# Layer 1's input projection by Strassen's algorithm in a two-layer encoder step

## The chip, the cores and the metric

The kernel runs on one core of a Trainium2 chip. The metric is the device time of one execution, in microseconds (us). The engines are named as in the profile: PE is TensorE (matmuls; PEld its weight loads), DVE is VectorE, ACT is ScalarE, POOL is GpSimd, SP is SyncE, whose queue issues all of this kernel's DMAs.

## The reference

One inference step of a two-layer trunk of width 1024 for 1024 prompt positions and 64 sample positions. Layer 0 is sparse attention beside a short convolution; the change leaves it alone. Layer 1, the "odd" mixer, is what matters here:

```python
def _odd_mixer(h, w_in, ws, bs, ln_g, ln_b, w_out):
    u, v, g = _split(h @ w_in, (SGU_DIM, SGU_DIM, SGU_DIM))
    u = jax.nn.gelu(u)
    v = _layernorm(jax.nn.gelu(v), ln_g, ln_b)
    ...
    s = jnp.einsum('gij,bnjgc->bnigc', wm, vc) + bs[:, :lc].T[None, None, :, :, None]
    s = s.reshape(nb, T, SGU_DIM)
    out = (u * s * jax.nn.silu(g)) @ w_out
    return out, v
...
        x = x + gate[:, None] * out
    ...
    return _rmsnorm(x, final_g), ...
```

`h` is the scaled and shifted RMS norm of x, `w_in` is 1024 x 3072, all data are float32. `wm` is a lower-triangular 128 x 128 matrix for each of 8 channel groups; it mixes positions inside blocks of 128. The normalised v of the 64 sample positions is an output of its own.

## The kernel before, in words

Activations lie transposed: channels on the 128 partitions in `KT` = 8 tiles, `TC` = 1088 columns for the positions (1024 prompt, 64 sample). Each float32 operand of a projection is split into a rounded high part and the rest, `ah` and `al` for the activations, `w_hi` and `w_lo` for the weights; a product is high x high + high x low + low x high, so three matmuls for each of the 8 channel tiles (`product`, L261). `project` makes one column tile of 128 outputs in three chunks of 364, 364 and 360 columns: 72 matmuls. `weights` loads a raw tile of 512 KB (L127), lets ACT round it (L252) and POOL subtract (L253); there are two raw buffers.

Layer 0 ends with its output projection (`out_projection`, three chunks `OUT_CHUNKS` of 448, 384 and 256 columns). Behind each matmul group DVE adds the gated result to the residual x (L1150), ACT squares it and POOL sums the squares; `rstd` makes the norm, and `h1` writes layer 1's `ah` (ACT, L1175) and `al` (POOL makes the float32 value, L1174, DVE subtracts, L1176). The residual stays in SBUF until the end.

`layer1` then runs 24 column tiles in the order v, g, u. For v: gelu, then PE transposes each 128 x 128 block into `vtok` (position on the partitions), copied out of PSUM by DVE (L1259); DVE does the layer norm (`layernorm`: statistics, scaling, times `ln_g`, plus `ln_b`). For g: silu into `gs`. `spatial` makes the mix, one group of channels at a time, by 8 + 1 matmuls, adds the bias and multiplies into `gs` (DVE, L1218, L1220). For u: gelu (ACT, L1289), multiplied into `gs` (DVE, L1290). At last `gs` is split into `ah` and `al` (L292, L293) and the second output projection runs, with `final` (L1182) behind it.

PSUM has eight banks, given out by tags: `pj`, `lg`, `pt` twice each, `av` and `x` once. Each engine runs its instructions strictly in the order in which they stand. That order is fixed when the program is built: for most of the program a scheduler places each instruction by estimated times, so an instruction written later may stand earlier.

Of the kernel before, what the change touches and what calls it, by code (L numbers as in the profile page):

```python
# [17 lines left out]
P = 128  # L18
# [77 lines left out]
OUT_KTS = (4, 5, 6, 7, 0, 1, 2, 3)  # L96

# [7 lines left out]
class Trunk:  # L105
# [1027 lines left out]
    def out_projection(self, l, ws, after):  # L1133
# [4 lines left out]
        for c in range(NCH):  # L1138
# [3 lines left out]
            acc = self.tmp.tile([P, CW], F32, tag="acc", name="acc", bufs=2)[:, 0:w]  # L1142
            for t in range(KT):
# [8 lines left out]
                if t == 0:  # L1152
                    nc.scalar.activation(acc, x[:, t, :], AF.Square)
                else:
                    sq = self.tmp.tile([P, CW], F32, tag="hf1", name="sq", bufs=2)[:, 0:w]
                    nc.scalar.activation(sq, x[:, t, :], AF.Square)  # L1156
                    if t < KT - 1 or c < NCH - 1:
                        nc.gpsimd.tensor_add(acc, acc, sq)  # L1158
                if c and t == 1:
                    after(c - 1, self.rstd("rstd", *accs[c - 1]))  # L1160
            accs.append((w, acc) if c < NCH - 1 else (w, acc, sq))
        after(NCH - 1, self.rstd("rstd", *accs[-1]))

    def h1(self, c, rb):
        nc = self.nc
        a0, b0 = OUT_CHUNKS[c]
        w = b0 - a0
        for kt in range(KT):
            t = self.tmp.tile([P, CW], F32, tag="t1", name="t1", bufs=2)[:, 0:w]
            hf = self.tmp.tile([P, CW], F32, tag="hf1", name="hf1", bufs=2)[:, 0:w]  # L1170
            nc.vector.tensor_mul(t, self.xc[c][:, kt, :], rb)
            for j, a, b in self.spans(c):
                sc, sh = self.modA[1][:, kt, j:j + 1], self.mod[1][:, kt, j:j + 1]
                nc.gpsimd.tensor_scalar(hf[:, a:b], t[:, a:b], sc, sh, op0=OP.mult, op1=OP.add)  # L1174
                nc.scalar.activation(self.ah[:, kt, a0 + a:a0 + b], t[:, a:b], AF.Identity, scale=sc, bias=sh)  # L1175
            nc.vector.tensor_sub(self.al[:, kt, a0:b0], hf, self.ah[:, kt, a0:b0])  # L1176
# [13 lines left out]
    def layernorm(self, n, pool):  # L1190
        nc = self.nc
        r = slice(0, P) if n < NBLK else slice(0, DEC)
        v = self.vtok[r, n, :]
        st = self.small.tile([P, 2, 6], F32, tag="bn", name="bn", bufs=2)
        mv = self.small.tile([P, 4], F32, tag="mv", name="mv", bufs=2)
        for i in range(2):
            nc.vector.bn_stats(st[r, i, :], v[:, i * 512:(i + 1) * 512])
# [7 lines left out]
    def spatial(self, g):  # L1205

        nc = self.nc
        pt = [self.bank("lg", "sgu_ps") for _ in range(2)]
        for n in range(NBLK):
            nc.tensor.matmul(pt[n // 4][:, (n % 4) * P:(n % 4 + 1) * P], self.vtok[:, n, g * P:(g + 1) * P],  # L1210
                             self.wm[:, g, :], start=True, stop=True)
        ps = self.bank("av", "sgus_ps")
        nc.tensor.matmul(ps[:, 0:DEC], self.vtok[0:DEC, NBLK, g * P:(g + 1) * P], self.wm[0:DEC, g, 0:DEC],
                         start=True, stop=True)
        gs = self.gs
        for a in range(2):
            s = self.big.tile([P, 512], F32, tag="sgu", name="sgu", bufs=1)
            nc.vector.tensor_add(s.rearrange("p (b c) -> p b c", c=P), pt[a].rearrange("p (b c) -> p b c", c=P),  # L1218
                                 self.bs[:, g, None, :].to_broadcast([P, 4, P]))
            nc.vector.tensor_mul(gs[:, g, a * 512:a * 512 + 512], gs[:, g, a * 512:a * 512 + 512], s)  # L1220
        s = self.small.tile([P, DEC], F32, tag="sgus", name="sgus", bufs=2)
        nc.vector.tensor_add(s, ps[:, 0:DEC], self.bs[:, g, 0:DEC])
        nc.vector.tensor_mul(gs[:, g, SO:SO + DEC], gs[:, g, SO:SO + DEC], s)

    def layer1(self):
# [3 lines left out]
        with ExitStack() as es:  # L1229
            gp = es.enter_context(self.pool("gates", "right"))  # L1230
            self.gs = gs = gp.tile([P, KT, TC], F32, name="gs")
            with ExitStack() as e2:
                b = e2.enter_context(self.pool("sgu", "right"))
                self.vtok = b.tile([P, NBLK + 1, D], F32, name="vtok")
                with self.pool("ln", "right") as lp:
                    self.lng, self.lnb = lp.tile([P, D], F32, name="lng"), lp.tile([P, D], F32, name="lnb")
                    with self.tc.issue_after(self.lastload):
                        self.load(self.lng, i["ln_g"].partition_broadcast(P))
                        self.load(self.lnb, i["ln_b"].partition_broadcast(P))
                    def gelu(t):  # L1240
                        def evac(c, ps):
                            nc.scalar.activation(gs[:, t, slice(*CHUNKS[c])], ps, AF.Gelu_apprx_tanh)
                        return evac


                    two = [self.weights(w1[t]) for t in range(2)]
                    for t in range(2):
                        self.project(two[t], gelu(t), range(NCH - 1))
                    for t in range(KT):
                        if t < 2:  # L1250
                            self.project(two[t], gelu(t), (NCH - 1,))
                        else:
                            self.project(self.weights(w1[t]), gelu(t))
                        for a in range(2):
                            pt = self.bank("lg", "v_ps")
                            for n in range(4):
                                nc.tensor.transpose(pt[:, n * P:(n + 1) * P],
                                                    gs[:, t, (4 * a + n) * P:(4 * a + n + 1) * P], self.ident)
# [12 lines left out]
                self.load(self.bs.rearrange("p g c -> p (g c)"), i["bs"].partition_broadcast(P))
                nc.gpsimd.affine_select(out=self.wm, in_=self.wm, compare_op=OP.is_ge, fill=0.0, base=0,
# [136 lines left out]
```

## Time and profile before

| What | us |
|---|---|
| median of 3 runs (lowest, highest) | 1114.68 (1113.75, 1117.47) |
| the profiled execution, its own time | 1114.53 |
| its span, first to last instruction | 1112.8 |
| layer 1's input projection starts, on PE | 689.63 |
| second output projection starts, on PE | 1004.25 |
| last matmul group of the output projection ends | about 1102 |

The granted PE clock was 0.994 of full speed over the span. In a timeline row the columns are start, duration, engine, line and operation; a matmul's duration overlaps the next one's, so the pace is the distance between starts. In a row of grouped instructions the columns are busy us, mean ns of one, and the engine's idle time before them with what ended it.

### The profile page before, as it was taken

How to read it: one execution, taken by the hardware profiler on the slowest of the kernel's cores; microseconds unless marked ns; L12 is line 12 of the kernel's file. 1: busy time of each engine (PE TensorE's matmuls, PEld its weight loads, DVE VectorE, ACT ScalarE, POOL GpSimd, SP SyncE). 2: the span in 40 equal slices, each digit the busy share in tenths (PEclk: the TensorE clock that was granted, in tenths of full speed). 3: DMA queues.
4: the chain of work that ended last, by engine and by line, in shares of the span. 5: the costliest groups of instructions: out<-in, count | busy, mean ns of one | idle time of the engine just before them, and what ended most of it. 6: DMA issues, size and time to landing. Idle time of an engine off the chain costs nothing.

```text
span 1112.8 us, 18831 instructions
## 1 busy us (share of the span) xinstructions
PE 1077.3 (97%) x7255; PEld 1042.8 (94%) x7255; DVE 645.6 (58%) x1614; ACT 535.4 (48%) x1019; POOL 440.9 (40%) x463
## 2 busy tenths in 40 slices
PE   5899999999999999999999999999999999999996
PEld 4889778999999989999999999999999999999996
DVE  5611789998887777677785344311492082346134
ACT  5643588766776687677785234411221112144111
POOL 1014223356675566455374356411242101264222
PEclk9999999999999999999999999999999999999998
DMA  9755601211010110000003501111112101130012
GB/s 370 285 199 170 238 30 57 79 39 56 22 39 24 63 48 21 20 20 20 20 20 108 205 1 38 39 38 38 39 48 95 39 20 39 46 125 20 1 67 95
DMA packets 25786, 81.84 MB, mean 74 GB/s; under 512 B 3040, under 2 KB 9440, under 8 KB 23264
## 3 DMA queue, kind: packets, MB, share of 16 engines
q1 hardware_dynamic: 25696, 80.63, 20.4%
q8 instruction: 57, 0.93, 0.3%
q14 instruction: 33, 0.27, 0.1%
HBM read 74.50 MB, written 6.12 MB: 72 GB/s over the span
## 4 chain that ended last, share of the span: by engine, by line
PE 88%; DVE 6%; ACT 4%; issue 2%; DMA 0%; POOL 0%; POOLq 0%; DVEq 0%; ACTq 0%
PE pj L261 44%; PE op L261 15%; PE pj L278 9%; PE av L728 3%; PE logit_ps L684 3%; PE p_ps L710 3%; PE ada_ps L165 2%; PE first L333 2%; PE sgu_ps L1210 1%; PE score_ps L448 1%; DVE cum L644 1%; PE score_ps L449 1%; DVE al L293 1%; ACT rel L451 1%; DVE bias L645 1%
## 5 line engine op out<-in xcount | busy, mean ns | idle before, releaser
L261 PE MATMUL pj<-ah,w_hi 128*128 128x364 f32 (+1 forms) x984 | 326.0, 331 | 1.0 <-ACT w_hi L252 1.0
L261 PE MATMUL pj<-al,w_hi 128*128 128x364 f32 (+1 forms) x984 | 323.8, 329 | 0.0
L261 PE MATMUL pj<-ah,w_lo 128*128 128x364 f32 (+1 forms) x984 | 323.0, 329 | 0.0
L253 POOL TENSOR_TENSOR w_lo<-w_raw,w_hi 128x1024 fp32r<-128x1024 f32 x63 | 155.5, 2469 | 345.8 <-ACT w_hi L252 343.8
L261 PEld LDWEIGHTS pj<-ah,w_hi 128*128 128x128 f32 x984 | 185.0, 188 | 2.0 <-ACT w_hi L252 1.3
L261 PEld LDWEIGHTS pj<-ah,w_lo 128*128 128x128 f32 x984 | 184.9, 188 | 0.3 <-issue 0.2
L261 PEld LDWEIGHTS pj<-al,w_hi 128*128 128x128 f32 x984 | 185.1, 188 | 0.0
L252 ACT ACTIVATE w_hi<-w_raw 128x1024 fp32r<-128x1024 f32 x68 | 71.8, 1058 | 108.0 <-PE pj L261 86.6
L550 DVE TENSOR_SCALAR_CACHE_REDUCE junk<-S,cand 128x512 bf16<-128x512 f32 (+5 forms) x142 | 119.0, 838 | 1.9
L261 PE MATMUL op<-al,w_hi 128*128 128x256 f32 (+2 forms) x344 | 112.0, 326 | 0.5 <-DVE al L293 0.5
L261 PE MATMUL op<-ah,w_hi 128*128 128x256 f32 (+2 forms) x344 | 112.3, 327 | 0.0
L261 PE MATMUL op<-ah,w_lo 128*128 128x256 f32 (+2 forms) x344 | 111.6, 326 | 0.0
L278 PE MATMUL pj<-ah,w_hi 128*128 128x364 f32 (+1 forms) x288 | 95.5, 332 | 0.0
L278 PE MATMUL pj<-ah,w_lo 128*128 128x364 f32 (+1 forms) x288 | 95.4, 331 | 0.0
L278 PE MATMUL pj<-al,w_hi 128*128 128x364 f32 (+1 forms) x288 | 95.2, 330 | 0.0
L577 ACT ACTIVATE junk<-S,cand 128x896 bf16<-128x896 f32 (+2 forms) x78 | 77.7, 996 | 30.3 <-DVE m L580 26.4
L1150 DVE SCALAR_TENSOR_TENSOR x<-op,mod,x 128x192 f32<-128x192 f32 (+2 forms) x64 | 30.2, 497 | 101.6 <-PE op L261 97.0
L691 POOL TENSOR_SCALAR S<-S,sm 128x128 f32<-128x128 f32 (+8 forms) x68 | 51.6, 763 | 67.5 <-DVE sm L690 54.8
L1158 POOL TENSOR_TENSOR acc<-acc,sq 128x448 f32<-128x448 f32 (+2 forms) x40 | 40.7, 1019 | 86.2 <-ACT sq L1156 85.5
L1156 ACT ACTIVATE sq<-x 128x448 f32<-128x448 f32 (+2 forms) x42 | 21.3, 506 | 96.5 <-DVE x L1150 92.9
L261 PEld LDWEIGHTS op<-al,w_hi 128*128 128x128 f32 x344 | 64.9, 189 | 2.6 <-DVE al L293 0.9
L261 PEld LDWEIGHTS op<-ah,w_hi 128*128 128x128 f32 x344 | 64.9, 189 | 1.7
(254 smaller groups left out, 2080.0 us busy)
## 6 DMA issues: line engine op xcount, KB each, us to landing
w_raw<-in_w SPq DMA_DIRECT2D x53, 512.0 KB, 3.4
ada<-in_ada_w SPq DMA_DIRECT2D x19, 1024.0 KB, 7.7
w_raw<-in_wo SPq DMA_DIRECT2D x16, 512.0 KB, 3.5
x<-in_x SPq DMA_DIRECT2D x8, 544.0 KB, 6.0
bo<-in_ada_w SPq DMA_DIRECT2D x4, 1024.0 KB, 6.8
x<-in_x SPq DMA_DIRECT2D x1, 1792.0 KB, 8.1
out_y<-x SPq DMA_DIRECT2D x1, 1792.0 KB, 6.6
x<-in_x SPq DMA_DIRECT2D x1, 1536.0 KB, 7.7
```

Of the source, the lines that this page charges most:

```text
L252: nc.scalar.activation(hi, raw, AF.Copy)
L253: (nc.gpsimd if lo_eng == "pool" else nc.vector).tensor_sub(lo, raw, hi)
L261: last = self.nc.tensor.matmul(ps, wt[:, kt, :], at[:, kt, c0:c1], start=n == 0, stop=n == len(mms) - 1)
L278: self.nc.tensor.matmul(ps, wt[:, kt, :], at[:, kt, a:b], start=kt == 0 and i == 0, stop=kt == KT - 1 and i == 2)
L550: V.tensor_scalar(junks[0][:, 0:SW[j]], self.S[:, span(j)], thr, 0.0, op0=OP.is_lt, op1=OP.add, accum_out=col(cv, j))
L577: nc.scalar.activation(junks[1][:, 0:SW[j]], self.S[:, span(j)], AF.Sign, scale=-1.0, bias=col(cand, j), accum_out=col(cv, j))
L684: nc.tensor.matmul(pt[:, 0:w], lhs, keys[i][:, t // 2, s], start=i == 0, stop=i == 1)
L691: self.lastnorm = nc.gpsimd.tensor_scalar(p, p, st[:, 3:4], 0.5, op0=OP.mult, op1=OP.mult).ins
L710: nc.tensor.transpose(pt[0:r, o:o + P], p[:, j * P:j * P + r], self.ident)
L728: self.lastav = nc.tensor.matmul(av[:, 0:m], self.vs[0:r, vbase + j, t // 2, :], part[0:r, x:x + m], start=j == 0 and i == 0, stop=(j + 1) ...
L1150: nc.vector.scalar_tensor_tensor(x[:, t, a:b], ps[:, a:b], self.mod[l][:, 16 + t, j:j + 1], x[:, t, a:b], op0=OP.mult, op1=OP.add)
L1158: nc.gpsimd.tensor_add(acc, acc, sq)
```

## The change

For 22 of the 24 column tiles of the input projection, two neighbouring tiles are made together by Strassen's algorithm (in the form with seven products). The weights of a pair are taken as a 2 x 2 matrix: two column tiles by the two halves of the channels (4 tiles of 128, `KH`). The activations are 2 x 2 too: halves of the channels by two neighbouring blocks of `Q` = 272 columns; there are two such groups of columns (`q`). Each of the seven products is a sum of weight quarters times a sum of activation quarters, over half the channels: 3 x 4 = 12 matmuls of 272 columns for each q. The results are added up in SBUF.

- The activation sums T1, T2, T3 and T4 are made once for all pairs: `sums` makes them in place of h, which `h1` now keeps in x's own buffers, and `sum_parts` splits them into high and low parts. T4 takes the place of a quarter of `ah` and `al`.
- For each pair DVE makes the four weight sums, ACT and POOL split seven weight quarters into four slots in turn (`pair_weights`).
- `pair` adds each product out of PSUM (DVE, 14 additions a pair; one copy for each q on ACT), applies gelu or silu in SBUF, and, for pairs from t = 12 on, multiplies into `gs` (`times`, DVE).
- The residual x is copied to DRAM behind its last update in layer 0's output projection (`spill`) and loaded again for layer 1's.
- The layer norm now only subtracts the mean and divides (ACT); `ln_g` multiplies behind the mix, and `ln_b` goes into the bias `bs` through the column sums of `wm` (`mix`, two more matmuls). The sample rows of v get both directly for the output.
- Layer 1's output weights for six of the eight tiles go into the places of T2, T1 and T3.

```diff
 def out_projection ...
+            if l == 0:
+                self.load(self.spill[c], x)
 def h1 ...
-                nc.gpsimd.tensor_scalar(hf[:, a:b], t[:, a:b], sc, sh, op0=OP.mult, op1=OP.add)
+                nc.gpsimd.tensor_scalar(x[:, kt, a:b], t[:, a:b], sc, sh, op0=OP.mult, op1=OP.add)
...
+    def sums(self):
+        V = self.nc.vector
+        for _, n, (c1, o1), (c2, o2) in self.half_pieces():
+            b11, b21 = (self.xc[c1][:, k:k + KH, o1:o1 + n] for k in (0, KH))
+            b12, b22 = (self.xc[c2][:, k:k + KH, o2:o2 + n] for k in (0, KH))
+            V.tensor_sub(b11, b12, b11)
+            V.tensor_sub(b12, b22, b12)
+            V.tensor_sub(b22, b22, b11)
+            V.tensor_sub(b21, b21, b22)
...
+    def pair_weights(self, s1, s2):
...
+        def parts(src):
+            self.turn += 1
+            w = pool.tile([P, 2, KH, P], F32R, tag=("whi0", "wlo0", "whi1", "wlo1")[self.turn % 4], name="p_w")
+            nc.scalar.activation(w[:, 0], src, AF.Copy)
+            nc.gpsimd.tensor_sub(w[:, 1], src, w[:, 0])
+            return w
...
+        yield parts(a11)
+        yield parts(a12)
+        t1 = total(0, V.tensor_add, a21, a22)
+        t2 = total(1, V.tensor_sub, t1, a11)
+        yield parts(t2)
+        yield parts(total(2, V.tensor_sub, a11, a21))
+        yield parts(t1)
+        yield parts(a22)
+        yield parts(total(0, V.tensor_sub, a12, t2))
+
+    def pair(self, t, dst, f, done=None, mid=None):
...
+        for n, (w, b) in enumerate(zip(ws, ("B11", "B21", "T2", "T3", "T1", "T4", "B22"))):
+            for q in range(2):
+                tag = ("pj", "lg", "pt")[n % 3]
+                ps = self.ps.tile([P, 512], F32, tag=tag, name="st", bufs=2)[:, 0:Q]
+                hi, lo = self.quarter(b, q)
+                mms = [(0, at, k) for k in range(KH) for at in (hi, lo)] + [(1, hi, k) for k in range(KH)]
+                for i, (p, at, k) in enumerate(mms):
+                    nc.tensor.matmul(ps, w[:, p, k, :], at[:, k, :], start=i == 0, stop=i == len(mms) - 1)
...
+                if n == 0:
+                    nc.scalar.activation(x12, ps, AF.Copy)
+                elif n == 1:
+                    V.tensor_add(x11, x12, ps)
+                    finish(0, s1)
...
+                else:
+                    V.tensor_add(x12, x12, ps)
+                    finish(0, s2)
...
 def layernorm ...
-        nc.vector.tensor_scalar(v, v, mv[r, 0:1], mv[r, 2:3], op0=OP.subtract, op1=OP.mult)
-        nc.vector.tensor_mul(v, v, self.lng[r])
-        nc.vector.tensor_add(v, v, self.lnb[r])
+        nc.vector.scalar_tensor_tensor(mv[r, 3:4], mv[r, 0:1], -1.0, mv[r, 2:3], op0=OP.mult, op1=OP.mult)
+        for i in range(2):
+            v = self.vtok[i][r, n, :]
+            nc.scalar.activation(v, v, AF.Identity, scale=mv[r, 2:3], bias=mv[r, 3:4])
 def spatial ...
+            nc.vector.scalar_tensor_tensor(o, p, self.lngb[:, 0, g:g + 1], b, op0=OP.mult, op1=OP.add)
+            if times:
+                nc.vector.tensor_mul(y, y, u)
 def layer1 ...
+        for t in range(2, KT, 2):
+            mid = transposes(t - 2, v)
+            v = [ring((t + n) % 4) for n in range(2)]
+            self.pair(t, v, AF.Gelu_apprx_tanh, mid=mid)
...
+        self.pair(KT, gsa, AF.Silu, mid=mix)
+        gsa += [ring(n) for n in range(2, 4)]
+        self.pair(KT + 2, gsa[2:], AF.Silu)
+        for g in range(4):
+            self.spatial(g, gsa[g], True)
...
+        for g in range(4, KT):
+            self.spatial(g, gs[g], False)
...
+        self.load(xc[0], self.spill[0])
...
+        for n, t in enumerate((*range(KT + 4, 2 * KT, 2), *range(2 * KT, 3 * KT, 2))):
+            def times(src, k, s):
+                nc.vector.tensor_mul(gs[t % KT + k][:, s], gs[t % KT + k][:, s], src)
+            self.pair(t, [tmp[:, n % 2 * 2 + k, :] for k in range(2)],
+                      AF.Silu if t < 2 * KT else AF.Gelu_apprx_tanh, done=times)
```

Up to the first chunk of `h1` every engine's instructions stand as before. Three places of DVE's order, each before and after:

**The end of h.** Before, DVE's last lower parts of h (L1176; `hf` is the float32 value) are followed at once by the copies of the first transposes.

```order
L1176 TENSOR_TENSOR al<-hf_7846,ah 128x256
L1176 TENSOR_TENSOR al<-hf_7854,ah 128x256
L1176 TENSOR_TENSOR al<-hf_7862,ah 128x256
L1259 COPY vtok<-v_ps 128x4x128 x3
L1263 COPY vtok<-vs_ps 64x128
```

Now DVE has the sums there (L1221 to L1223; `x_6978` is the last chunk of x, `x_6980` the one before) and the low parts of T3, T2 and T4, then the first pair's first addition (L1304) and weight sums (`p_s`).

```order
L1181 TENSOR_TENSOR al<-x_6978,ah 128x256
L1221 TENSOR_TENSOR x_6978<-x_6978 128x1024
L1222 TENSOR_TENSOR x_6978<-x_6978,x_6980 128x1024
L1223 TENSOR_TENSOR x_6980<-x_6980,x_6978 128x4x256
L296 TENSOR_TENSOR T3l<-x_6978,T3h 128x4x256
L296 TENSOR_TENSOR T2l<-x_6978,T2h 128x4x256
L296 TENSOR_TENSOR al<-x_6980,ah 128x4x256
L1304 TENSOR_TENSOR ring<-ring,st 128x272
L1263 TENSOR_TENSOR p_s<-p_raw 128x512 x2
L1332 COPY vtok_8087<-v_ps 128x4x128 x2
```

Six operations of 1024 columns have come between the last part of h and the weight sums, and the copies of the transposes have moved behind them.

**The end of the norm.** Before, DVE's order runs through the scaling of the last blocks (L1201 to L1203) into the mix (L1218).

```order
L1201 TENSOR_SCALAR vtok<-vtok,mv 128x1024 x2
L1202 TENSOR_TENSOR vtok<-vtok,lng 128x1024
L1198 BN_AGGR mv<-bn 128x2
L1202 TENSOR_TENSOR vtok<-vtok,lng 128x1024
L1203 TENSOR_TENSOR vtok<-vtok,lnb 128x1024
L1199 TENSOR_SCALAR mv<-mv 128x1
L1203 TENSOR_TENSOR vtok<-vtok,lnb 128x1024
L1201 TENSOR_SCALAR vtok<-vtok,mv 128x1024
L1202 TENSOR_TENSOR vtok<-vtok,lng 128x1024
L1203 TENSOR_TENSOR vtok<-vtok,lnb 128x1024
L1218 TENSOR_TENSOR sgu<-sgu_ps,bs 128x512
```

Now the statistics (L1344 to L1348) stand between the additions of a pair (L1315, L1318), and the last of them behind the mix's first operation (L1372).

```order
L1344 BN_STATS bn<-vtok_8087 128x6
L1344 BN_STATS bn<-vtok_8088 128x6
L1318 TENSOR_TENSOR ring<-ring,st 128x272
L1348 SCALAR_TENSOR_TENSOR mv<-mv 128x1
L1345 BN_AGGR mv<-bn 128x2
L1346 TENSOR_SCALAR mv<-mv 128x1
L1318 TENSOR_TENSOR ring<-ring,st 128x272
L1348 SCALAR_TENSOR_TENSOR mv<-mv 128x1
L1372 SCALAR_TENSOR_TENSOR sgu<-sgu_ps,lngb,misc 128x512
L1345 BN_AGGR mv<-bn 128x2
L1374 TENSOR_TENSOR ring<-ring,sgu 128x512
```

Three operations of 1024 columns for each block have left DVE, and the rest has moved to just before the mix.

**The end of a gate pair.** Before, DVE had one multiplication for each chunk of a tile, `u` being a new buffer each time.

```order
L1290 TENSOR_TENSOR gs_7874<-gs_7874,u_9744 128x364
L1290 TENSOR_TENSOR gs_7874<-gs_7874,u_9772 128x364
L1290 TENSOR_TENSOR gs_7874<-gs_7874,u_9800 128x360
L1290 TENSOR_TENSOR gs_7874<-gs_7874,u_9834 128x364
L1290 TENSOR_TENSOR gs_7874<-gs_7874,u_9862 128x364
```

Now, at the end of the pair t = 12 (the results of products 5 and 6 are `st_9874` to `st_9922`, and `st_10001` belongs to the next pair):

```order
L1315 TENSOR_TENSOR u_9688<-u_9688,st_9874 128x272
L1466 TENSOR_TENSOR gsb_9625<-gsb_9625,u_9688 128x272
L1315 TENSOR_TENSOR u_9688<-u_9688,st_9890 128x272
L1466 TENSOR_TENSOR gsb_9625<-gsb_9625,u_9688 128x272
L1318 TENSOR_TENSOR u_9688<-u_9688,st_9906 128x272
L1466 TENSOR_TENSOR gsb_9625<-gsb_9625,u_9688 128x272
L1318 TENSOR_TENSOR u_9688<-u_9688,st_9922 128x272
L1466 TENSOR_TENSOR gsb_9625<-gsb_9625,u_9688 128x272
L1263 TENSOR_TENSOR p_s_10206<-p_raw_10187 128x512
L1304 TENSOR_TENSOR u_9688<-u_9688,st_10001 128x272
```

Each addition is now followed by the multiplication of its own result, with a function on ACT between the two, and the addition that frees the last bank (L1318) stands behind a multiplication.

More of the change, by code (lines that the diff above doesn't have):

```diff
@@ L1207, in spatial @@
+    def spatial(self, g, gs, times):
         nc = self.nc
-        pt = [self.bank("lg", "sgu_ps") for _ in range(2)]
+        vt, c = self.vtok[g // 4], slice(g % 4 * P, (g % 4 + 1) * P)
+        pt = [self.ps.tile([P, 512], F32, tag="lg", name="sgu_ps", bufs=2) for _ in range(2)]
         for n in range(NBLK):
-            nc.tensor.matmul(pt[n // 4][:, (n % 4) * P:(n % 4 + 1) * P], self.vtok[:, n, g * P:(g + 1) * P],
-                             self.wm[:, g, :], start=True, stop=True)
-        ps = self.bank("av", "sgus_ps")
@@ L1213, in spatial @@
[L1213 to L1225, printed above, removed]
+            nc.tensor.matmul(pt[n // 4][:, (n % 4) * P:(n % 4 + 1) * P], vt[:, n, c], self.wm[:, g, :],
+                             start=True, stop=True)
+        ps = self.ps.tile([P, 512], F32, tag="x" if g % 2 else "av", name="sgus_ps", bufs=1)
@@ L1226, in layer1 @@
+    def layer1(self, es):
         nc = self.nc
@@ new lines, in layer1, with ring, gelu, evac @@
+        r1 = es.enter_context(self.pool("sums", "right"))
+        self.T = {t: [r1.tile([P, KH, 2 * Q], F32R, tag=f"T{t}{x}", name=f"T{t}{x}") for x in "hl"] for t in (1, 2, 3)}
+        def ring(n):
+            return r1.tile([P, TC], F32, tag=f"ring{n}", name="ring")
+        v = [ring(n) for n in range(2)]
+        def gelu(t):
+            def evac(c, ps):
+                nc.scalar.activation(v[t][:, slice(*CHUNKS[c])], ps, AF.Gelu_apprx_tanh)
+            return evac
+        two = [self.weights(w1[t]) for t in range(2)]
@@ new lines, in layer1, with mix @@
+        gsa = [ring(n) for n in range(2)]
+        mid = transposes(KT - 2, v)
+        def mix():
+            mid()
+            for a in range(2):
+                ps = self.ps.tile([P, 512], F32, tag="av" if a else "x", name="r_ps", bufs=1)
+                nc.tensor.matmul(ps, ones, misc[:, 2, a * 512:a * 512 + 512], start=True, stop=True)
+                for g in range(4 * a, 4 * a + 4):
+                    nc.vector.scalar_tensor_tensor(self.bs[:, g, :], ps[:, g % 4 * P:(g % 4 + 1) * P],
+                                                   self.lngb[:, 1, g:g + 1], self.bs[:, g, :], op0=OP.mult, op1=OP.add)
+            for n in (NBLK, *range(NBLK)):
+                self.layernorm(n)
+            for h in range(2):
+                x = slice(h * 512, h * 512 + 512)
+                nc.vector.tensor_mul(lng[0:DEC, x], lng[0:DEC, x], self.vtok[h][0:DEC, NBLK, :])
+            nc.vector.tensor_add(lng[0:DEC], lng[0:DEC], lnb[0:DEC])
+            self.load(self.o["cv"], lng[0:DEC])
@@ new lines, in layer1 @@
+        ws = [self.weights(i["wo1"][t], "pool", place=r1.tile([P, 2, KT, P], F32R, tag=f"T{(2, 1, 3)[t // 2]}{'hl'[t % 2]}",
+                                                             name="w_1") if t < 6 else None) for t in range(KT)]
+        for c in range(NCH):
+            s = slice(*OUT_CHUNKS[c])
+            for t in range(KT):
+                self.split(self.ah[:, t, s], self.al[:, t, s], gs[t][:, s])
+        for c in range(1, NCH):
+            xc.append(r2.tile([P, KT, w[c]], F32, tag=f"v{c % 2}", name=f"x{c}"))
+            self.load(xc[c], self.spill[c])
```

225 lines of the change are left out of this document (148 added, 77 removed).

## The prediction

> **What bounds the kernel now.** I read the page's busy shares and slices first, then who waited for whom on TensorE, then the chain and the timeline around layer 1.
>
> ```profile
> span 1112.8 us, 18831 instructions
> PE 1077.3 (97%) x7255; PEld 1042.8 (94%) x7255; DVE 645.6 (58%) x1614; ACT 535.4 (48%) x1019; POOL 440.9 (40%) x463
> PE   5899999999999999999999999999999999999996
> DVE  5611789998887777677785344311492082346134
> POOL 1014223356675566455374356411242101264222
> PEclk9999999999999999999999999999999999999998
> ...
> PE rstd L226 <- ACT sq L1156: 1.1, 1, 1.1
> PE rstd L232 <- POOL rs L230: 1.0, 1, 1.0
> PE op L261 <- DVE al L293: 0.5, 1, 0.5
> ```
>
> TensorE is busy in every slice but the first two and the last, at a full clock, and the waits behind the middle of the program are 0.5 us in one place and 2.1 us in the tail. VectorE and POOL have idle time in most slices of layer 1 (25 to 37). So layer 1's input projection costs what its matmuls cost in start-to-start time. A matmul's own mean (331 ns) is not that: matmuls overlap. I take starts.
>
> ```profile
> 689.63 4.51 PE pj L261 x27
> ...
> 715.23 0.87 PE v_ps L1257 x8
> ...
> 798.28 59.89 PE pj L261 x360
> ...
> 917.69 80.73 PE pj L261 x484
> ...
> 1004.25 0.36 PE L261 MATMUL op<-ah,w_hi 128*128 128x448 f32 x1
> ```
>
> The projection runs from 689.63 to 1004.25 us, 314.6 us. Its stretches without anything else give 59.89/360 = 0.1664 and 80.73/484 = 0.1668 us per matmul; I use **0.1665**. 24 tiles of 72 matmuls make 1728 x 0.1665 = 287.7 us; of the other 27 us, 72 transposes take 8 (0.87/8 each) and the spatial mix, with the switches into it and out, 19. The change keeps both in number.
>
> **The change, part by part.** *Matmuls.* A pair of tiles was 2 x 72 = 144 matmuls of 364 or 360 columns; it becomes 7 products x 2 halves x 12 = 168 of 272 columns. Eleven pairs: 1584 go, 1848 come. The trace has no 272-column matmul. Its nearest row is the last chunk of the output projections, 256 columns, a weight load before each as here:
>
> ```profile
> 676.75 0.28 PE L261 MATMUL op<-ah,w_lo 128*128 128x256 f32 x1
> ...
> 680.95 0.28 PE L261 MATMUL op<-ah,w_lo 128*128 128x256 f32 x1
> ...
> 1089.79 0.28 PE L261 MATMUL op<-al,w_hi 128*128 128x256 f32 x1
> ...
> 1094.71 0.28 PE L261 MATMUL op<-ah,w_hi 128*128 128x256 f32 x1
> ```
>
> The first pair of rows spans 36 intervals (0.1167 us each), the second 41 (0.1200 us). From their mean, 0.1184 at 256 columns, to 0.1665 at 364 the slope is 0.00045 us a column, so 272 columns take 0.1184 + 16 x 0.00045 = **0.1255 us**. Scaling the two rows by columns alone gives 0.1240 and 0.1275, my bounds. Old 1584 x 0.1665 = 263.7; new 1848 x 0.1255 = 231.9 (229.2 to 235.6). That is **-31.8 us** (-34.5 to -28.1). A pair falls from 24.0 to 21.1 us. That is nearly the seven eighths by which the columns of a pair fall (144 x 362.7 to 168 x 272): by these rows a column costs about the same at both lengths.
>
> The Trainium skill would price this otherwise: "TensorE: Matmul & The Clock Gate", section Back-to-back issue gap, has a warm gap of N/2.4 + 2.5 ns, 115.8 ns at 272 columns, by which the new matmuls would take 214 us and the kernel some 18 us less than I forecast. By the same rule 256 columns would take 109 ns, and the rows above show 117 to 120; the measurement decides.
>
> *Work that TensorE doesn't see.* Two column-sum matmuls for the norm's bias cost 0.5 us (512 columns at the rate above, twice). Residual to DRAM and back: each chunk is copied out behind its last update and comes back before chunk 0, 1, 2 of the output projection.
>
> ```profile
> out_y<-x SPq DMA_DIRECT2D x1, 1792.0 KB, 6.6
> w_raw<-in_wo SPq DMA_DIRECT2D x16, 512.0 KB, 3.5
> 709.04 0.43 DVE L1176 TENSOR_TENSOR al<-hf,ah 128x256 fp32r<-128x256 f32 x1 [0.88 <-POOL hf L1174]
> ```
>
> The largest chunk took 6.6 us to write. POOL now writes h into x in place and must wait for that copy; for the last chunk it is issued near 690 us and h starts at 699 (the last lower part is at 709.04), so it is covered: nothing. The way back has 30 us or more ahead of each use. Weights come in the same bytes.
>
> *Per-pair side work.* VectorE gets 14 additions from PSUM, 4 weight sums of 512, and in the six gate pairs 8 multiplications; POOL 7 subtractions of 512 (half of L253's 2.39 us: 1.2 each, 8.4 us); ScalarE 7 copies of 512 (half of 1058 ns each), 2 copies and 8 functions, about 8 us.
>
> ```profile
> L1150 DVE SCALAR_TENSOR_TENSOR x<-op,mod,x 128x384 f32<-128x384 f32 x8 | 4.9, 617 | 24.2 <-PE op L261 24.2
> ...
> L1150 DVE SCALAR_TENSOR_TENSOR x<-op,mod,x 128x192 f32<-128x192 f32 x9 | 3.8, 418 | 16.6 <-PE op L261 16.6
> ...
> L252 ACT ACTIVATE w_hi<-w_raw 128x1024 fp32r<-128x1024 f32 x37 | 39.1, 1058 | 88.2 <-PE pj L261 74.3 <-DMA w_raw<-in_wo 10.9 <-PE op L261 3.0
> ...
> 940.55 0.48 ACT L1289 ACTIVATE u<-pj 128x364 f32<-128x364 f32 x1 [3.50 <-PE pj L261]
> 941.05 0.54 DVE L1290 TENSOR_TENSOR gs<-gs,u 128x364 f32<-128x364 f32 x1 [3.44 <-ACT u L1289]
> ...
> 945.56 2.39 POOL L253 TENSOR_TENSOR w_lo<-w_raw,w_hi 128x1024 fp32r<-128x1024 f32 x1 [9.56 <-ACT w_hi L252]
> 945.88 2.47 DVE L1290 TENSOR_TENSOR gs<-gs,u 128x360 f32<-128x360 f32 x1 [4.28 <-ACT u L1289]
> ```
>
> 272 columns from PSUM lie between 418 and 617 ns: 0.50. A multiplication of 364 took 0.54 alone, so 0.44 at 272; 512 columns 0.69. A gate pair is 14 x 0.50 + 4 x 0.69 + 8 x 0.44 = 13.3 us of VectorE, of 21.1. But the last row shows a multiplication of two SBUF operands stretched to 2.47 us while POOL subtracts. Six PSUM banks in turn give 9 us of slack inside a pair; at a pair's end product 6 and the next product 0 share two banks, and an addition has only one half-product, 1.5 us, to free one. I take 2 us over ten joins (0 to 6).
>
> *First pair.* VectorE makes the sums and the low parts of T1 to T4 in the layer's first 30 us. TensorE reaches the first T product after 144 ordinary matmuls (24.0 us), some 1 us of transposes and norm columns and two products (6.0): about 720.8. VectorE ends h near 709.5 as before, or up to 3 us later, then has six operations of 1024 columns, and only then the weight sums that four of the next products need.
>
> ```profile
> L352 DVE TENSOR_TENSOR al<-hf,ah 128x1088 fp32r<-128x1088 f32 x8 | 10.3, 1293 | 10.6 <-ACT hf L347 10.6
> ```
>
> Six at 1.2 us end at 717 to 720; one PSUM addition, two weight sums (1.4) and ScalarE's 0.55 follow: 721 to 723. I take a stall of 2 us (0 to 6).
>
> *Norm and mix.* Scaling moves from VectorE to ScalarE and into the mix, but the norm now stands in one pair's 21 us, just ahead of the mix.
>
> ```profile
> L1220 DVE TENSOR_TENSOR gs<-gs,sgu 128x512 f32<-128x512 f32 x16 | 13.0, 813 | 0.8 <-DVE sgus L1222 0.3
> ...
> L1218 DVE TENSOR_TENSOR sgu<-sgu_ps,bs 128x512 f32<-128x512 f32 x16 | 11.1, 692 | 48.7 <-PE sgu_ps L1210 47.9
> ...
> L1197 DVE BATCH_NORM_STATS2 bn<-vtok 128x6 f32<-128x512 f32 x16 | 10.2, 677 | 0.0
> ...
> 892.00:917.00 25.00, 25.00 (x180) 23.87 (x180) 23.34 (x45) 2.78 (x5) 2.36 (x1) 1.00 0.07 22
> ```
>
> From the last transposes to the mix's end VectorE has 18 statistics (12.2), some 8 us of small operations on them, on the bias and on the sample rows (an estimate: some 45 of them), 17 additions (8.5), 5 weight sums (3.5), 16 x 0.69 + 8 x 0.81 from the mix and its small ones (20.2): about 52 us. TensorE has 4.5 us of the last transposes' products, one pair (21.1), the mix (19) and one product (3.0): 47.6 us. In the old mix VectorE was busy 23.34 of 25 us, and TensorE filled the gaps with projection matmuls; now fewer can fill, since product 1 needs the banks of the mix. I take 4 us (0 to 8).
>
> *Start of the output projection.* Its weights go into the places of T2, T1, T3, free only during the last pair; two raw buffers in turn, each 3.5 us of transfer, 1.06 of ScalarE and 2.39 of POOL, give one weight per 3.5 us or so against 24 x 0.2025 = 4.9 us of use.
>
> ```profile
> 1019.83 0.36 PE L261 MATMUL op<-al,w_hi 128*128 128x448 f32 x1
> ...
> 1023.88 0.36 PE L261 MATMUL op<-ah,w_hi 128*128 128x448 f32 x1
> ```
>
> (20 intervals of 448 columns.) The first tile that TensorE asks for is ready within about 1 us of its use: 1 us (0 to 4).
>
> **Sum.** -31.8 + 0.5 + 2 + 2 + 4 + 1 = -22.3 us. Against the profiled execution's own 1114.53 us (its span is 1112.8; the median of the runs is 1114.68) that is **1092 us**. With all bounds: 1080.5 to 1111.
>
> **Rivals.** *Slower: VectorE sets the pace of the gate pairs.*
>
> ```profile
> L1290 DVE TENSOR_TENSOR gs<-gs,u 128x364 f32<-128x364 f32 x16 | 15.7, 979 | 28.2 <-ACT u L1289 28.1
> ```
>
> It is in order; each multiplication stands behind the function of the addition just ahead (0.48 us for 364 columns) and behind POOL's subtraction. If it waits for all of them, a gate pair is 13.3 + 8 x 0.48 + 7 x 1.2 = 25.5 us instead of 21.1; six pairs add 26 us: 1118. The point is 24.8 us a pair, from which the gain is gone. For it: the 2.47 us row. Against: these 16 of the 24 old multiplications averaged 979 ns, between 0.54 and 2.47, and POOL is at work for 8.4 us of 21. Chance 0.09. The Trainium skill speaks for it: "SBUF — State Buffer", section SBUF: two separate sides, calls the port pair that VectorE and GpSimd share an exclusive lock held for a whole instruction, also for a VectorE operation with two SBUF inputs. The trace agrees: 2.47 us beside 2.39.
>
> *Faster: 272 columns cost what 256 do at best,* 0.1167 us. 1848 x 0.1167 = 215.7 us, 16 less: 1076. Against: 364 and 360 columns already differ from 256 by their columns. Chance 0.04.
>
> *Half the gain goes into joins:* first pair, norm and output start together beyond their bounds, 1107 to 1115. For it: the order was laid out for other durations. Chance 0.07. My forecast, 1080 to 1107, has **0.80**.
>
> **Chances and range.** A measurement of this kernel tells about 0.3% (3.3 us) from no change. Faster: 0.80 + 0.04 + 0.03 of the joins' case = 0.87. Same: 0.04 + 0.01 = 0.05. Slower: 0.08. Range 1080 to 1107, which leaves 0.2 out.
>
> **What would show it.** 272-column matmuls starting every 0.124 to 0.1275 us; gate pairs of 21 to 22 us; TensorE's waits for VectorE of some us near 721, at the mix, and of parts of a us at pair ends. Wrong it is if a pair takes 24 us, if VectorE is busy throughout the gate pairs, or if POOL waits for the copies of x near 700.

## The result, and the profile after

The changed kernel takes 1095.52 us (median of 4 runs, 1094.69 to 1096.83) against 1114.33 (1113.75 to 1117.47): ratio 0.9827, 95% interval 0.9806 to 0.9848. The profiled spans are 1094.1 and 1112.8 us, 18.7 less. 1092 was forecast, in a range of 1080 to 1107.

The page of the changed kernel: span, busy times, and slices of TensorE, VectorE and the clock.

```profile
span 1094.1 us, 20011 instructions
PE 1050.8 (96%) x7523; PEld 1013.6 (93%) x7523; DVE 738.5 (67%) x1849; ACT 592.5 (54%) x1152; POOL 493.5 (45%) x519
PE   4899999999999989999999999989999999999996
DVE  5610789998887786777787445685568876667134
PEclk9899999999999999999999999999999999999998
```

VectorE's slices in the projection (26 to 36) rose from 0 to 4 tenths, with two of 8 and 9, to 5 to 8, and TensorE still has only one slice below nine there. From the chain of what ended last, a stretch of matmuls without anything else; then what TensorE waited for from the start of layer 1's projection to the end.

```profile
859.93 115.80 PE st L1291 x924
...
PE st L1291 <- ACT p_w L1257: 2.6, 1, 2.6
PE op L264 <- DVE al L296: 1.8, 1, 1.8
PE sgu_ps L1359 <- DVE sgu L1372: 1.1, 4, 0.5
...
PE op L264 <- ACT ah L295: 0.8, 1, 0.8
PE pj L264 <- DVE al L1181: 0.7, 2, 0.6
PE st L1291 <- ACT ring L1390: 0.6, 1, 0.6
PE sgu_ps L1359 <- DVE gsb L1372: 0.4, 1, 0.4
```

924 products' matmuls, five and a half pairs, in 115.80 us are 0.1253 us each, and none of the rows below is a wait inside a gate pair or between two pairs. The 2.6 us stand before the first T product of the first pair, the 0.7 and 0.6 just ahead of that pair, the 1.8 and 0.8 at the start of the output projection, the two of `sgu_ps` in the mix.

Where the time went, from TensorE's rows: the time from each start to the next, summed by kind over the projection (689.47 to 1004.25 us before, 691.21 to 983.08 after), so that a wait counts with the matmul ahead of it. (689.47 us is the first matmul; the 689.63 in the table of the kernel before is the start of a row of the chain.)

| us | before | after |
|---|---|---|
| matmuls of ordinary tiles | 290.2 | 26.3 |
| matmuls of products | - | 237.6 |
| spatial mix | 17.2 | 20.3 |
| transposes, norm columns | 7.4 | 6.8 |
| column sums | - | 0.9 |
| projection | 314.8 | 291.9 |
| ahead of it | 689.5 | 691.2 |
| behind it, to the span's end | 108.55 | 111.0 |

Two of these rows need a second reading, at the places where the kind changes:

```profile
810.85 1.02 PE L1437 MATMUL r_ps<-misc,ones 128*128 128x512 f32 x2
811.31 0.69 PE L1291 MATMUL st<-al,p_w 128*128 128x272 f32 x1
811.84 0.28 PE L1291 MATMUL st<-ah,p_w 128*128 128x272 f32 x1
```

From the column sum's start to the second product matmul behind it pass 0.99 us, of which one product matmul is 0.13: a column sum (one matmul, two records) costs 0.86 us, both together 1.7. The 0.9 in the table leaves out what shows up as the late start of the matmul behind. In the same way each switch out of the mix puts 0.08 us with the projection's matmul behind it. There were 17 such switches before and there are four now, so 1.1 of the 3.1 us by which the mix's row grew is only counted elsewhere, and the mix grew by 2.0.

### The profile page after: what moved, and what is told of

Its sections match the earlier page's. It is cut to its first block, busy times and chain, and to the rows that moved or that the text cites. A ratio compares the mean times of both kernels' runs of the same rounds, so it can differ in the third digit from the quotient of the medians.

```text
span 1094.1 us, 20011 instructions
## 1 busy us (share of the span) xinstructions
PE 1050.8 (96%) x7523; PEld 1013.6 (93%) x7523; DVE 738.5 (67%) x1849; ACT 592.5 (54%) x1152; POOL 493.5 (45%) x519
## 4 chain that ended last, share of the span: by engine, by line
PE 83%; DVE 9%; ACT 3%; issue 2%; DMA 1%; POOL 1%; SPq 0%; POOLq 0%; DVEq 0%; ACTq 0%
PE st L1291 20%; PE pj L264 20%; PE op L264 15%; PE pj L281 9%; PE av L731 3%; PE logit_ps L687 3%; PE p_ps L713 3%; PE ada_ps L168 2%; PE first L336 2%; PE score_ps L451 1%; DVE al L296 1%; DVE cum L647 1%; PE score_ps L452 1%; DMA x<-in_x 1%; DVE bias L648 1%
## 5 line engine op out<-in xcount | busy, mean ns | idle before, releaser
L264 PE MATMUL pj<-ah,w_hi 128*128 128x364 f32 (+1 forms) x456 | 150.3, 331 | 1.0 <-ACT w_hi L255 1.0
L264 PE MATMUL pj<-al,w_hi 128*128 128x364 f32 (+1 forms) x456 | 150.3, 330 | 0.7 <-DVE al L1181 0.7
L264 PE MATMUL pj<-ah,w_lo 128*128 128x364 f32 (+1 forms) x456 | 149.2, 329 | 0.0
L1291 PE MATMUL st<-ah,p_w 128*128 128x272 f32 x704 | 137.3, 290 | 0.6 <-ACT ring L1390 0.6
L1291 PEld LDWEIGHTS st<-ah,p_w 128*128 128x128 f32 x704 | 111.7, 188 | 1.7 <-ACT ring L1390 0.9
L281 PE MATMUL pj<-ah,w_lo 128*128 128x364 f32 (+1 forms) x288 | 95.7, 332 | 0.0
L281 PE MATMUL pj<-ah,w_hi 128*128 128x364 f32 (+1 forms) x288 | 95.5, 332 | 0.0
L281 PE MATMUL pj<-al,w_hi 128*128 128x364 f32 (+1 forms) x288 | 95.3, 331 | 0.0
L1291 PE MATMUL st<-al,p_w 128*128 128x272 f32 x352 | 92.8, 291 | 0.0
L264 PEld LDWEIGHTS pj<-ah,w_hi 128*128 128x128 f32 x456 | 85.6, 188 | 2.0 <-ACT w_hi L255 1.3
L264 PEld LDWEIGHTS pj<-al,w_hi 128*128 128x128 f32 x456 | 85.7, 188 | 1.3 <-DVE al L1181 1.3
L264 PEld LDWEIGHTS pj<-ah,w_lo 128*128 128x128 f32 x456 | 85.6, 188 | 0.2 <-issue 0.2
L264 PE MATMUL op<-ah,w 128*128 128x448 f32 (+2 forms) x336 | 82.4, 330 | 0.8 <-ACT ah L295 0.8
```

Source lines behind the costliest of these rows:

```text
L264: last = self.nc.tensor.matmul(ps, wt[:, kt, :], at[:, kt, c0:c1], start=n == 0, stop=n == len(mms) - 1)
L281: self.nc.tensor.matmul(ps, wt[:, kt, :], at[:, kt, a:b], start=kt == 0 and i == 0, stop=kt == KT - 1 and i == 2)
L1291: nc.tensor.matmul(ps, w[:, p, k, :], at[:, k, :], start=i == 0, stop=i == len(mms) - 1)
```

## The experiments

All are edits of the changed kernel. A kernel that was run once is read by the stretches of its profile, not by its one time, for a reason that comes last.

**The first pair.** Three kernels went after the 2.6 us in front of the first T product, where the weight sums stand behind the last low parts on VectorE.

```diff
-  self.l1.tile([P, KH, P], F32, tag=f"S{n}", name="p_s")   # memory of the residual
+  self.s1.tile([P, KH, P], F32, tag=f"S{n}", name="p_s")   # s1 = r1, free from the layer's start
```

The mix's `sgu` and the last projection's columns, which shared that memory, move with the sums.

> Edit: the four weight sums of a pair get places of their own that are free from the layer's start, so VectorE makes the first pair's before the low parts of T3, T2 and T4 instead of behind them. In the changed kernel TensorE stands still for 2.61 us at 727.99 in front of the first T product. Theory (the weight sums stand in the queue behind the last low parts): the product starts straight after the two products before it, the 2.61 us goes to under 0.7 us, the span falls from 1094.1 to about 1091.5 us. Rival (the T data themselves are late, by VectorE and POOL holding each other up): T3's low part still ends near 724 and T2's near 725, the extra sums push them back, the stall stays at 2 us or more and the span at 1094.

> Edit: as sums_early, and the copies of the first two transposed tiles out of PSUM go from VectorE to ScalarE (4 of 512 columns and 2 of 128, some 3.2 us of VectorE). Moving the weight sums alone took away the 2.61 us wait at the first T product and brought 3.24 us of waits for those copies (730.8 to 742.2 us). Theory (VectorE is behind by some 3 us in this pair, whichever of its results is queued last): with 3.2 us less of work on it both waits go, the stretch from the first product to the mix's first matmul falls from 117.4 to about 114.5 us. Rival (the order only chooses which wait is seen, and the lock with POOL's subtractions, which make VectorE's 1024-column rows 2.2 to 2.3 us instead of 1.22, keeps it late): a wait of 1.5 us or more stays at the T products, 116 us or more.

In `rows`, for the first two tiles: `nc.scalar.activation(o, p, AF.Copy)` for `nc.vector.tensor_copy(o, p)`. The third kernel has the sums early, the output weights' low parts on VectorE (below), and

```diff
-            if n == 3 and mid:
+            if n == (6 if t == 2 else 3) and mid:
```

> Output weights' low parts on VectorE; weight sums in places of their own; and the first two tiles are transposed behind product 6 of the first pair instead of product 3, so that their copies are no longer asked for while VectorE is behind. Theory (VectorE's lag in the first pair is some 3 us that slack later in the pair can take up): no wait over 1 us from 718 us to the mix, 2 to 2.5 us less than with the output weights' low parts alone, some 5 us less than the changed kernel: about 1090.3 us. Rival (the lag comes out somewhere else again, as in the two tries before): 2.5 us or more of waits in that stretch, no faster than with the low parts alone.

TensorE's waits from 716 to 747 us at the latest, of the three kernels in this order:

```profile
PE vs_ps L1334 <- DVE vtok L1332: 2.9, 2, 1.6
...
PE v_ps L1331 <- DVE vtok L1332: 0.3, 1, 0.3
```

```profile
PE vs_ps L1338 <- ACT vtok L1334: 3.7, 1, 3.7
```

```profile
PE st L1291 <- DVE ring L1318: 1.8, 1, 1.8
```

The 2.6 us went each time, and 3.2, 3.7 and 2.0 us came at another place (with the 1.8 us of the last row goes a wait of 0.2 us for `L1304`). From the first product to the mix's first matmul: 117.4 us in the changed kernel, 118.3, 119.9 and 117.2 in these. (1.5 us of the 119.9 are a halved clock behind the wait, as in the last section: fifteen product matmuls start 0.227 us apart. Without that the second kernel would be at 118.4, still far from the 114.5 of its theory.) The first theory (VectorE's queue) told the wait rightly and the time wrongly; the second was wrong; the third was too. The last kernel shows what stands behind them. VectorE, then the DMA queue of SP:

```profile
735.89 0.42 DVE L1313 TENSOR_TENSOR ring<-ring,st 128x272 f32<-128x272 f32 x1
740.54 0.86 DVE L1263 TENSOR_TENSOR p_s<-p_raw 128x512 f32<-128x512 f32 x1 [4.23 <-DMA p_raw<-in_w]
```

```profile
731.76 0.51 SPq L130 DMA_DIRECT2D misc<-in_ln_g  x1
...
733.58 0.43 SPq L130 DMA_DIRECT2D misc<-in_bs  x1
734.30 25.44 SPq L130 DMA_DIRECT2D p_raw<-in_w  x8
```

VectorE stands idle 4.2 us for the second pair's raw weights. These are issued behind four constants of the norm and mix (1.5 MB), which wait for the residual's memory, free only after the last low part (T4). That part ended at 731.7 us here, since in VectorE's queue it now stood behind a weight sum, and at 726.1 in the changed kernel, whose wait for the same transfer is 1.6 us. So each edit that moved the sums ahead held up the constants and the next weights. The constants' part in it is the transfer: the raw weights issued at 734.30 landed at 740.45, 6.1 us later, and those issued at 743.78 landed in 2.6. Their issue would hardly have been sooner, because the buffer that they go into is read by the first pair's last weight sum, which ended at 734.23. Loading the constants later, which only the mix needs, was not tried.

**The start of the output projection.**

```diff
-        ws = [self.weights(i["wo1"][t], "pool", place=...
+        ws = [self.weights(i["wo1"][t], "dve", place=...
```

> Edit: the low parts of layer 1's output weights are subtracted on VectorE instead of POOL. In the changed kernel the start of that projection costs 3.0 us of waits of TensorE for VectorE's low parts and ScalarE's high parts, while VectorE operations beside POOL's subtraction take 2.3 to 2.6 us instead of 0.4 to 0.8. Lock theory (the two engines hold each other up): VectorE's rows at 979 to 995 us fall back to 0.45 to 0.8 us, the eight subtractions add 8 x 1.2 us over some 40 us, the waits fall to under 1 us, span about 1092. Load rival (VectorE simply has too much at this place): the added 3.6 us of the first three subtractions come on top, waits 5 us or more, span 1096 or more.

> The output weights' low parts on VectorE, timed: the part behind the projection was 108.0 us instead of 111.0. Lock theory: 3.0 us (0.27%) faster than the changed kernel. Rival (the first look was a lucky execution, its 1092.1 us due to the clock at the start): within 1 us of the changed kernel.

VectorE and POOL in the changed kernel, then VectorE with the edit:

```profile
979.27 2.43 DVE L1466 TENSOR_TENSOR gsb<-gsb,u 128x272 f32<-128x272 f32 x1
...
990.26 2.60 DVE L1466 TENSOR_TENSOR gsb<-gsb,u 128x272 f32<-128x272 f32 x1
```

```profile
979.00 2.40 POOL L256 TENSOR_TENSOR w<-w_raw,w 128x1024 fp32r<-128x1024 f32 x1 [1.08 <-ACT w L255]
985.36 3.89 POOL L256 TENSOR_TENSOR w<-w_raw,w 128x1024 fp32r<-128x1024 f32 x1 [3.96 <-ACT w L255]
990.10 2.46 POOL L256 TENSOR_TENSOR w<-w_raw,w 128x1024 fp32r<-128x1024 f32 x1 [0.85 <-ACT w L255]
```

```profile
978.88 0.43 DVE L1466 TENSOR_TENSOR gsb<-gsb,u 128x272 f32<-128x272 f32 x1
...
988.55 1.22 DVE L256 TENSOR_TENSOR w<-w_raw,w 128x1024 fp32r<-128x1024 f32 x1
989.68 0.43 DVE L1466 TENSOR_TENSOR gsb<-gsb,u 128x272 f32<-128x272 f32 x1
```

A multiplication of 272 columns takes 0.43 us, and 2.4 to 2.6 beside a subtraction on POOL. With that work on VectorE both waits are gone, and the part behind the projection takes 108.0 us (107.97 again) instead of 111.0. The lock theory (each engine holds the other up) holds to the tenth: more work on the busier engine, and 3 us less.

Timed beside the changed kernel on one chip, against the kernel before:

> The changed kernel again, unedited, as the base for the two below on the same chip: 1095.5 us, within 1 us. It also bears on why what lies ahead of the projection came 1.7 us later than before in its first profile: in other runs of the same code this part was 2.2 to 2.9 us shorter, where the granted clock at 34 to 42 us stayed at 1.00 instead of 0.59. If that is chance, single times spread over some 2 to 3 us.

| | us | ratio, 95% interval |
|---|---|---|
| changed kernel, again | 1095.79 (1094.54 to 1096.39) | 0.9822, 0.9808 to 0.9835 |
| output weights on VectorE | 1092.95 (1092.68 to 1094.32) | 0.9800, 0.9786 to 0.9813 |
| and sums early, transposes late | 1092.39 (1089.49 to 1095.04) | 0.9792, 0.9772 to 0.9811 |

The second is 2.8 us faster than the first; its theory said 3.0. The third cannot be told from the second, so its theory, 1090.3 us, is not borne out.

**The lock in the gate pairs.** `pair_weights` subtracts on VectorE where t >= KT + 4, beside the edit above.

> In the six pairs behind the mix the seven low parts of weights, 512 columns each, go from POOL to VectorE (and the output weights' too, as above): 7 x 0.68 = 4.8 us more on VectorE in a gate pair that has 14.3 to 14.8 busy of 21.0, so about 18.5 to 19, and no POOL subtraction that could hold it up. My reading of the prediction's rival (VectorE has room up to the pair's 21 us): gate pairs stay at 21.0 to 21.3 us, span within 1.5 us of the kernel with the output weights alone on VectorE. Rival (in its order of queue VectorE waits for ScalarE and TensorE and is the bound well below full): gate pairs of 22 us or more, 6 us or more on the span.

Two stretches of 21 us in the gate pairs (columns: length, then TensorE, its loads, VectorE, ScalarE and POOL busy), in the changed kernel and here:

```profile
900.00:921.00 21.00, 21.00 (x170) 21.00 (x169) 14.66 (x28) 9.68 (x19) 9.56 (x8) 1.00 0.16 52
921.00:942.00 21.00, 21.00 (x170) 21.00 (x169) 14.25 (x27) 8.13 (x17) 9.35 (x8) 1.00 0.16 51
```

```profile
900.00:921.00 21.00, 21.00 (x170) 21.00 (x169) 15.80 (x33) 9.24 (x19) 0.00 (x0) 1.00 0.15 51
921.00:942.00 21.00, 21.00 (x170) 21.00 (x169) 15.76 (x33) 8.07 (x18) 0.00 (x0) 1.00 0.15 52
```

TensorE stays full, and the stretch from the mix's last matmul to the output projection is 123.4 us in both: the rival falls. (The mix itself took 20.9 us instead of 20.3.) I had expected 18.5 to 19 us of VectorE, and it is 15.8. It took on 4.8 us of subtractions, and its busy time rose by 1.1 and 1.5 in the two stretches, so some 3.3 to 3.7 us a pair of its time had been POOL's lock, hidden under TensorE.

**The pace of a matmul.** In the products, all but the first matmul of each group, with 256 and 192 for z; the other columns are left out:

```diff
+                    z = Q if i == 0 else 256
-                    nc.tensor.matmul(ps, w[:, p, k, :], at[:, k, :], ...
+                    nc.tensor.matmul(ps[:, 0:z], w[:, p, k, :], at[:, k, 0:z], ...
```

> Leaves out 16 of the 272 columns in 11 of the 12 matmuls of each half product of the pairs (1694 of 1848 matmuls at 256 columns). Theory (a matmul is paced by its columns, 0.00045 us each): 1694 x 16 x 0.00045 = 12.2 us less, span about 1082, start to start 0.118 us. Rival (at this length the weight load or a fixed gap sets the pace, 0.125 us whatever the columns): span within 2 us of 1094.

> Leaves out 80 of the 272 columns in 11 of 12 matmuls of the pairs, so that TensorE's share of a gate pair falls from 21 to about 15.1 us, with VectorE, ScalarE and POOL doing all they did. At 256 columns the matmuls followed their columns (622 in 74.00 us, 0.119). It asks how far VectorE (14.3 to 14.8 us of a gate pair) is from being the bound. My reading of the prediction's rival (VectorE becomes the bound only when each multiplication waits for all ahead of it): gate pairs shrink to 15.1 to 17 us, with short waits for VectorE. The rival as priced (25.5 us a pair from VectorE's queue): gate pairs stay near 21 us, no shorter than in the changed kernel.

From the chains, first of 256, then of 192 columns, and one wait of the first:

```profile
874.88 74.00 PE st L1292 x622
...
PE op L264 <- POOL w L256: 3.9, 1, 3.9
```

```profile
855.54 40.41 PE st L1292 x359
```

0.1190 and 0.1126 us on average, one in twelve still at 272 columns. From start to start between two matmuls of the same length, in the gate pairs, it is 0.1253 us at 272 columns, 0.1179 at 256 and 0.1095 at 192. From 272 to 256 a column is worth 0.00046 us, as forecast; over the next 64 it is 0.00013 each. The theory holds at this change's length and stops somewhere below. The span at 256 fell by 6.6 us, not 12.2: the projection by 10.4, of which 3.7 came back behind it, where the output weights are now late on POOL. At 192 a gate pair takes 19.0 to 19.3 us, not the 15.1 to 17 I expected. Its 168 matmuls at 0.1126 us are 18.9, so TensorE still sets it, and how much further VectorE would go, it can't show.

**The norm and the mix.** The first kernel's edit is `self.layernorm(NBLK)` for the loop over all blocks; the second's is below; the third normalises, scales and shifts on VectorE as before the change.

> Leaves out the normalisation of the eight blocks of prompt rows (its statistics, small operations and the scaling on ScalarE); the 64 sample rows keep theirs. In the changed kernel the spatial mix waits about 3.3 us in small pieces for its own evictions on VectorE, 842 to 854 us, with VectorE full from 814 on. Theory (the norm's some 15 us of VectorE in one pair's time makes the mix late): with it gone the waits fall to under 1 us and the span by 3 us or more. Rival (the mix itself, two banks in turn and 3.2 us of VectorE a group against 1.3 us of TensorE, sets the waits): 2 us or more of waits stay and the span falls by less than 1.5 us.

> Edit: the 12 multiplications of the first four groups of the spatial mix (6.3 us of VectorE) go to POOL, which is idle there. Without the prompt rows' norm the mix's waits fell only from 1.8 to 0.7 us. Theory (the mix's own evictions on VectorE set the waits): the mix, 21.2 us from its first to its last matmul, shortens by 1 to 2 us. Rival (POOL's operation takes twice as long and holds VectorE up): as long as before or longer.

```diff
-                nc.vector.tensor_mul(y, y, u)
+                nc.gpsimd.tensor_mul(y, y, u)
```

> Undoes one part of the change: the rows are normalised, scaled and shifted on VectorE (three operations of 512 columns twice per block, as in the kernel before) instead of scaled on ScalarE with weights and bias folded into the mix; the column sums go too. Theory (VectorE is full from 814 to 860 us and the mix waits for it): 9 blocks x 6 operations x about 0.6 us = 32 us more on VectorE, less some 8 us of fold work, so the mix ends some 20 us later and the span is 1112 to 1118, all the gain of the matmuls gone. Rival (the work spreads over idle time of the pair before and behind): less than 8 us more, below 1102.

TensorE's waits in the mix, without the norm and with POOL's multiplications:

```profile
PE sgu_ps L1359 <- DVE gsb L1372: 0.4, 1, 0.4
PE sgu_ps L1359 <- DVE sgu L1372: 0.2, 1, 0.2
```

```profile
PE sgu_ps L1359 <- DVE sgu L1372: 1.0, 1, 1.0
PE sgu_ps L1359 <- DVE gsb L1372: 0.6, 1, 0.6
```

Without the norm the waits fell from the 1.5 us of the rows shown first to 0.6, and the mix from 20.3 to 19.4 us by the sum from start to start: the norm is worth 0.9 us of the 2.0 that the mix grew. With the multiplications on POOL the waits stayed at 1.6, and by the same sum the mix took 19.9 us instead of 20.3: a gain of 0.4, short of the theory's 1 to 2, though not the nothing of the rival. What makes up the rest of the 2.0 is not settled.

With the fold undone, two stretches of the windows and TensorE's longest wait:

```profile
814.00:836.00 22.00, 20.18 (x158) 19.77 (x158) 21.57 (x44) 5.58 (x12) 10.80 (x10) 1.00 0.14 37
836.00:860.00 24.00, 10.54 (x55) 9.41 (x53) 23.56 (x58) 1.99 (x5) 4.26 (x4) 0.67 0.00 1
...
PE sgu_ps L1362 <- DVE vtok L1354: 13.3, 4, 5.1
```

The span is 1121.9 us, 28 more than with the fold, past the 1112 to 1118 expected and the rival's 1102. VectorE is full, TensorE is busy 10.5 of 24 us, and its clock falls to 0.67 in its waits. In this order of work the products' gain exists only with the fold.

## Why the prediction was right, point by point

| term, us | forecast | measured |
|---|---|---|
| matmuls | -31.8 | -32.1 |
| column sums | +0.5 | +1.7 |
| pair joins | +2 | 0 |
| first pair | +2 | +4.6 |
| norm and mix | +4 | +2.0 |
| start of the output projection | +1 | +2.5 |
| ahead of the projection | 0 | +1.7 |
| transposes, switches between kinds, rounding of the paces (what is left) | 0 | +0.9 |
| sum | -22.3 | -18.7 |

VectorE at the end of h, the last of its low parts and two of the six operations behind it:

```profile
716.52 0.43 DVE L1181 TENSOR_TENSOR al<-x,ah 128x256 fp32r<-128x256 f32 x1 [0.22 <-POOL x L1179]
...
719.37 2.20 DVE L1223 TENSOR_TENSOR x<-x,x 128x1024 f32<-128x1024 f32 x1
721.50 2.32 DVE L296 TENSOR_TENSOR T3l<-x,T3h 128x1024 fp32r<-128x1024 f32 x1
```

- **Matmuls.** Interpolated 0.1255 us, measured 0.1253: 1848 of them are 231.6 us. The gap rule of the Trainium skill ("TensorE: Matmul & The Clock Gate", section Back-to-back issue gap) would have had 0.1158; the page gives it for an isolated matmul, not for a stream with a weight load before each. The two kernels with fewer columns show why a line through the neighbours served: 272 lies on the part where columns count. That it came out to 0.2% is in part luck: the prediction's two rows of 256 columns differ by 3% (0.1167 and 0.1200), and nothing said that the new matmuls would lie in the middle.
- **Column sums: mis-sized by a factor of three.** 512 columns were priced at the rate of the projections' rounded operands. These operands are plain float32, and one such matmul costs 0.86 us. The price stood in the kernel before: the mix's matmuls have 128 columns of plain float32 and two records each, 0.11 us apart, so 0.22 us a matmul.
- **Pair joins.** Two banks and 1.5 us were enough; there is no wait at a join. The 2 us forecast for them was a guess between 0 and 6. It and the 2 us too many for the mix hid about half of what came dearer elsewhere, and that is luck.
- **First pair: the term that was mis-sized most.** Waits of 2.6, 0.7 and 0.6 us and the slower first starts behind them make 4.6. Two steps failed. h was to end near 709.5 us or up to 3 later, and ended at 717: VectorE's queue has low parts and sums of 1024 columns between its steps. And the sums were taken at 1.2 us each, where `L1223` and the low part behind it take 2.2 to 2.3 beside POOL's subtractions. That h's delay comes from its neighbours on VectorE and POOL is read from the trace and wasn't tried alone. The three experiments add what the sum didn't contain: behind VectorE stands the residual's memory, and behind that the next pair's weights.
- **Norm and mix.** Inside the bounds, at half the forecast, which put the whole of it to VectorE's load in that pair; the run without the norm leaves that load 0.9 us.
- **Start of the output projection.** The forecast asked only when the first weight is ready. It was; VectorE's low parts were late, by POOL's subtractions. The lock was weighed for the gate pairs, where it stays hidden, and not here, where TensorE waits for VectorE.
- **VectorE's rival, 1118.** A gate pair takes 21.0 us with VectorE at 14.3, and with POOL's subtractions moved onto VectorE (4.8 us there) at 15.8. The lock is real, as the Trainium skill says in "SBUF — State Buffer", section SBUF: two separate sides; the trace agrees with 2.43 us beside 2.40. It did not decide there.
- **Ahead of the projection** nothing was forecast and 1.7 us came. 1.0 of it was there when TensorE leaves the attention (602.5 instead of 601.5 us), ahead of all that the change touches, and is chance (last section). The other 0.7 arose in layer 0's output projection and is not chance: from its first matmul to layer 1's projection it is 112.5 us before, 113.2 in the changed kernel and in every kernel made from it that has the fold, and 112.5 where the fold is undone. There is no wait in it; the matmuls themselves start further apart, 0.1200 us instead of 0.1167 at 256 columns. So the same matmul has two paces in these kernels, and what chooses between them stays open.

## What to carry to other kernels

Look for the lock between VectorE and POOL where TensorE waits for VectorE: there, eight subtractions moved to the busier engine were worth 3 us, and in stretches that TensorE paces the same lock costs nothing. When a wait is moved and the time stays, follow the idle engine behind it to its DMA, and that DMA to the memory it waits for. Price a new matmul from measured neighbours on both sides and of its own operand type, and shorten matmuls only while their columns still set the pace.

## What the runs showed of the hardware

The clock. TensorE alone, from 34 to 42 us (columns: length, busy, granted clock, DMA), in the kernel before, the changed kernel, and the changed kernel again:

```profile
34.00:42.00 8.00, 7.00 (x47) 0.79 0.99 395
```

```profile
34.00:42.00 8.00, 7.33 (x29) 0.59 1.02 414
```

```profile
34.00:42.00 8.00, 7.78 (x99) 1.00 1.02 416
```

This is behind a wait of some 3 us at 31 to 35 us. The projection then starts at 689.5, 691.2 and 688.2 us, and over all profiles of kernels with this start at 688.2 to 693.3. The same comes back in the first pair, in the changed kernel run again:

```profile
724.97 0.40 PE L1291 MATMUL st<-T1h,p_w 128*128 128x272 f32 x1 [2.59 <-ACT p_w L1257]
...
726.89 0.43 PE L1291 MATMUL st<-T3l,p_w 128*128 128x272 f32 x1
727.11 0.43 PE L1291 MATMUL st<-T3h,p_w 128*128 128x272 f32 x1
727.34 0.43 PE L1291 MATMUL st<-T3l,p_w 128*128 128x272 f32 x1
```

Start to start is 0.225 us here instead of 0.125, for some 3 us, at a granted clock of 0.53 from 725.5 to 728 us, and this stretch costs 1.5 us more (118.9 instead of 117.4 from first product to mix). The wait of 2.6 us was followed by half the clock in some executions and not in others of the same code. The Trainium skill, "TensorE: Matmul & The Clock Gate", section What's actually happening, lets the clock fall to half after an idle window of about 3.4 us that runs free of the program. The halving and the spread between executions agree; a wait of 2.6 us was enough here. So a short stall may cost half as much again, and two profiles of one kernel differ ahead of any edit by 3.0 us (the changed kernel) and 3.7 us (output weights on VectorE). That is why kernels run once are read by stretches above.
